# A two-pass transformer layer on one core: the turn of the first value block is put later, and the last SwiGLU step is cut down to its bank-freeing adds

## The chip, the core and the metric

The kernel runs on one core of one Trainium2 chip. The number that counts is the device time of one execution, in microseconds (us). The kernel before the change took 1397.57 us (median of 3 runs, 1396.01 to 1397.66).

The engines are named as the profile names them: PE is TensorE, which does the matmuls; PEld is its weight loading; DVE is VectorE, ACT is ScalarE, POOL is GpSimd, and SP is the queue from which nearly all transfers between memory and the core are issued. Each engine works through its own list of instructions in order; an instruction waits until what it reads is written and until the buffer that it writes is free. All tiles lie in the core's main memory, SBUF, but for the matmuls' results: these go into eight banks of a smaller one, PSUM, each 128 by 512 numbers of 32 bits. A bank can be written afresh only when another engine has read out what lay in it.

## The reference

One layer with 1024 tokens and 1024 features. With the sizes of this case only the first of the two kinds of attention is run:

```
h = x
hn = rms_norm(h, norm_mix);  h = h + stick_breaking_attention(hn, sb_w_in, sb_w_out)
h = h + (silu(a) * b) @ ffn_w_out      where a, b = split(rms_norm(h, norm_ffn) @ ffn_w_in)
gate = sigmoid(rms_norm(h, norm_ple) @ ple_w_gate)
h = h + gate * (p @ ple_w_proj)
return rms_norm(h, final_norm)

# stick-breaking attention, 16 heads of 64, strictly causal:
#   A[t,s] = sigmoid(z_ts) * prod over s<j<t of (1 - sigmoid(z_tj)),   out = A @ v
```

The SwiGLU's inner width is 2816, which is 22 blocks of 128.

## The kernel before, in words

Everything is kept transposed: features lie on the 128 partitions, tokens along the rows, in two halves of 512. Every matmul operand is split into a high part (a rounded cast, made by ACT) and a low part (the rest, a subtraction on DVE or POOL), and each product is three matmuls: high by high, high by low, low by high (`mm3`, lines 126 to 129). For weights this is `w_split` (line 98): line 106 casts on ACT, and line 107 picks the engine that subtracts in line 108.

**The attention** goes over 8 pairs of heads. While the attention of one pair is computed, the projections of the next pair (queries, keys, values: `sel` 0, 1, 2, each in two halves `h`) are fed in between, a few matmuls at a time, by the generator `proj_steps` (line 321). One step of it is one `mm3`; eight steps (`kt` 0 to 7) fill a bank of the kind `b_pj`, which DVE then reads out. The values of a pair are first turned by PE, 128 by 128 at a time: `turn_v` (line 308) does four such turns with the unit matrix into a bank `b_tp` (line 314), and ACT and DVE copy the result into the tile `V` (lines 317, 318). What is turned is `dv`, a difference of neighbouring values that DVE makes in line 305. These turns are not issued at once: they are put on the list `late`, and `proj_steps` empties the list when it comes to `kt == 3`, whichever block that is in. The banks `b_tp` and the score banks `b_z` share one ring of four. The scores are made by `s_atom` (PE in lines 407 and 408, the sigmoid on ACT in line 410, a scan on DVE in line 417), and the probabilities are turned by `a_atom` (PE in line 430, ACT and DVE in lines 439 and 440).

**The SwiGLU's first product** goes over 22 steps `k`, each with seven products of four `mm3` (a Strassen-like scheme that saves one in eight): `ps1`, `ps5`, `ps6`, `ps7`, `ps2`, `ps4` and `ps3`, in this order on PE, each in a bank of its own out of eight in a ring (`mb`). DVE adds them up into the tiles `q1`, `u2`, `u4` and `c22` (line 634, `add`); an add that reads a product from its bank frees that bank. The four sums are multiplied by the norm's factor (line 828, `scaled`, on DVE or POOL), and `glu` (line 830) makes silu(a) times b of two of them at a time: a sigmoid on ACT (832), two products on DVE (833, 834), and a store to memory from SP (835). `glu` of the second token half runs one step later, as `tail`.

**The second product** follows directly: for each half of the tokens, 22 out steps, each with eight `mm3`, one into each of eight banks (`pm[0]` to `pm[7]`). An out step needs the block's weights, split by `w_split`, and the stored activations, loaded again (`act_dma`) and split (`act_split`: cast in line 626, subtraction in line 627). The first two weight blocks and the first two activations are split within the last SwiGLU step, `k == NFF - 1`, so that out step 0 can begin when the last product is done. The ring of banks goes on across this border: the third group of out step 0 takes the bank of `ps5`, the sixth that of `ps2`, the seventh that of `ps4`, and the eighth that of `ps3`.

All of this is written out by hand in one order (no scheduler), from the second product of the attention on.

Of the kernel before, what the change touches and what calls it, by code (L numbers as in the profile page):

```python
# [19 lines left out]
NFF = 22  # L20
# [20 lines left out]
def tile_trunk(ctx: ExitStack, tc: tile.TileContext, xT, pT, gains, ident, w_qkv, w_o, w_fi, w_fo, w_g, w_p, outT):  # L41
# [54 lines left out]
    def w_split(k):  # L96
        if k < lim[0] and k in raws:
            n = order[k][1]
            t = raws.pop(k)
            if len(order[k]) > 2 and order[k][2]:  # L100
                hi = xp.tile([P, T], F32R, name=f"whi{k}", tag="X").rearrange("p (k m) -> p k m", k=KT)
                lo = xp.tile([P, T], F32R, name=f"wlo{k}", tag="X").rearrange("p (k m) -> p k m", k=KT)
            else:
                hi = wp.tile([P, KT, P], F32R, name=f"whi{k}", tag="whi", bufs=2)
                lo = wp.tile([P, KT, P], F32R, name=f"wlo{k}", tag="wlo", bufs=2)
            nc.scalar.copy(hi[:, :n, :], t[:, :n, :])  # L106
            eng = nc.gpsimd if k < N1 or k >= len(order) - 3 else nc.vector
            eng.tensor_tensor(lo[:, :n, :], t[:, :n, :], f(hi[:, :n, :]), op=ALU.subtract)  # L108
            parts[k] = (hi, lo)

# [58 lines left out]
    with ExitStack() as c1:  # L169
# [152 lines left out]
        def proj_steps(pr, sels=(0, 1, 2)):  # L322
            for sel in sels:
                wh, wl = w_next()
                if sel == 0:
                    alloc_qk(pr)
                for h in range(2):
                    hs = slice(h * 512, h * 512 + 512)
                    ps = jb()
                    for kt in range(KT):  # L330
                        if kt == 3:
                            while late:
                                late.pop(0)()
                        mm3(ps, wh[:, kt, :], wl[:, kt, :], xh[kt][:, hs], xl[kt][:, hs], kt == 0, kt == KT - 1)
                        if kt == KT - 1:
                            if sel == 0:
                                evac_q(pr, ps, h)
                            elif sel == 1:
                                evac_k(pr, ps, h)
                            else:  # L340
                                v = evac_v(pr, ps, h)
                                late.append(lambda pr=pr, v=v, h=h: turn_v(pr, v, h))
                        yield
# [278 lines left out]
    def act_split(i):  # L622
        if i < 2 * NFF and i not in acts:
            t = araw.pop(i)
            a = duo(xp, f"act{i}", "X", None)
            nc.scalar.copy(a[:, 0, :], t)
            nc.vector.tensor_tensor(a[:, 1, :], t, f(a[:, 0, :]), op=ALU.subtract)
            acts[i] = a

    with ExitStack() as c2:  # L630
# [196 lines left out]
        def scaled(t, h, eng=nc.vector):  # L827
            eng.tensor_tensor(t, t, rstd2[:, HS[h]], op=ALU.mult)  # L828
# [14 lines left out]
        for k in range(NFF):  # L843
            w = wc
            wc, todo = fi_prep(k + 1)
            fi_load(k + 2)
            if k >= NFF - 2:
                for i in range(2):
                    w_load(n_fi + 2 * (k + 2 - NFF) + i)
                act_dma(k + 2 - NFF)  # L850
            ps1 = prod(w["A11"], "B11")
            q1 = tmp("q1")
            nc.scalar.copy(q1, ps1)
            if tail:
                tail()
            ps5 = prod(w["S1"], "T1")
            if k == 0:
                ps2 = prod(w["A12"], "B21")
            if k:
                todo[0]()  # L860
                todo[1]()
            ps6 = prod(w["S2"], "T2")
            u2 = tmp("u2")
            add(u2, ps6, q1)
            u4 = tmp("u4")
            add(u4, ps5, u2)
            if k:
                todo[2]()
            if k == NFF - 1:
                act_split(0)  # L870
                w_split(n_fi)
            ps7 = prod(w["S3"], "T3")
            add(u2, ps7, u2)
            c22 = tmp("c22")
            add(c22, ps5, u2)
            if k == 0:
                yy = stats_sum(cp, mb(), acc2, 0, KT)
                for q in range(3):
                    todo[q]()
            todo[3]()  # L880
            if k:
                ps2 = prod(w["A12"], "B21")
            add(q1, ps2, q1)
            if k:
                scaled(c22, 1, nc.gpsimd)
                scaled(q1, 0)
            todo[5]()
            if k == NFF - 1:
                act_split(1)
            ps4 = prod(w["A22"], "T4")  # L890
            add(u2, ps4, u2)
            if k:
                scaled(u2, 0, nc.gpsimd)
            todo[4]()
            if k:
                glu(k, 0, q1, u2)
            if k == NFF - 1:
                w_split(n_fi + 1)
                act_dma(2)
            ps3 = prod(w["S4"], "B22")  # L900
            if k == 0:
                for h in range(2):
                    stats_spread(mb(), yy[:, 4 * h:4 * h + 4], rstd2, 512 * h, 4)
                scaled(c22, 1, nc.gpsimd)
                scaled(q1, 0)
                scaled(u2, 0, nc.gpsimd)
                glu(k, 0, q1, u2)
            add(u4, ps3, u4)
            scaled(u4, 1)

            def tail(k=k, u4=u4, c22=c22):
                glu(k, 1, u4, c22)

        tail()


    p3 = ctx.enter_context(tc.tile_pool(name="p3", bufs=1, reuse_waits="tile"))
# [26 lines left out]
    for h in range(2):  # L944
        pm = [None] * KT
        tail = []
        for k in range(NFF):
            i = h * NFF + k
            act_dma(i)
            act_split(i)  # L950
            act_dma(i + 1)
            act_dma(i + 2)
            wh, wl = w_next()
            if h == 1 and 2 <= k < 10:
                parts3(k - 2, 0)
            act_split(i + 1)
            a = acts.pop(i)
            if h == 1 and k in WGK:
                wg.append(w_next())
            if k < NFF - 2:  # L960
                for m in range(KT):
                    if k == 0:
                        pm[m] = mb()
                    mm3(pm[m], wh[:, m, :], wl[:, m, :], a[:, 0, :], a[:, 1, :], k == 0, False)
            else:
                tail.append((wh, wl, a))
        res = []
        for m in range(KT):
            t = tmp("h2")
            nc.sync.dma_start(t, h2_d[m][h])  # L970
            res.append(t)
        for m in range(KT):
            for q, (wh, wl, a) in enumerate(tail):
                mm3(pm[m], wh[:, m, :], wl[:, m, :], a[:, 0, :], a[:, 1, :], False, q == 1)
            residual(m, h, pm[m], res[m])
# [139 lines left out]
```

## Time and profile before

| what | value |
|---|---|
| median of 3 runs | 1397.57 us |
| the profiled execution's own time | 1397.2 us |
| its span, first to last instruction | 1395.4 us |
| PE busy | 1359.3 us, 97% of the span |
| DVE busy | 1006.8 us, 72% |
| ACT busy | 609.2 us, 44% |
| POOL busy | 406.4 us, 29% |
| granted PE clock, mean | 0.993 of full speed |

The profile is of one execution. An engine counts as busy while an instruction of its own runs. The timeline lists instructions by their start; in brackets stands how long the engine had been idle and who let it go on. The granted clock is the share of full speed at which PE was allowed to run in a stretch: 1.0 is 2.4 GHz, 0.5 is 1.2 GHz. Starts of PE's matmuls lie closer together than their durations, since they are pipelined; what counts is the distance from one start to the next.

### The profile page before, as it was taken

What the parts mean: (1) busy time and instruction counts of PE and PEld (TensorE: products, weight loads), DVE (VectorE), ACT (ScalarE), POOL (GpSimd) and SP (SyncE); (2) the same over time, 40 slices, a digit from 0 to 9 for tenths busy, and PEclk for the clock granted to TensorE, in tenths of its full rate; (3) what the DMA queues carried; (4) which work ended last, traced back from release to release, by engine and by line L of the source; (5) the groups of instructions that cost most, each with busy time, mean ns of one, the idle gap of its engine ahead of it and who ended that gap; (6) DMA issues with size and microseconds to landing.
All of it is one profiled execution on the core that took longest, in us unless ns stands there. A gap on an engine that the chain in (4) does not pass through costs nothing. (4 is left out here: it accounts for less than half of the span.)

```text
span 1395.4 us, 17612 instructions
## 1 busy us (share of the span) xinstructions
PE 1359.3 (97%) x6620; PEld 1135.1 (81%) x6620; DVE 1006.8 (72%) x1305; ACT 609.2 (44%) x1082; POOL 406.4 (29%) x280
## 2 busy tenths in 40 slices
PE   8899999999999999999999999999999999999996
PEld 6788888888888878878888888888877888888896
DVE  6778788787887875677888888888884336645775
ACT  6555665655566664443232323222322223433333
POOL 2221322312222501234445444545440000301321
PEclk9999999999999999999999999999999999999998
DMA  5101111111111571442221222221235445555123
GB/s 188 41 31 46 46 46 46 46 34 43 46 46 61 182 263 46 162 146 79 91 85 58 84 91 91 91 71 66 91 106 188 138 156 208 168 175 181 31 71 104
DMA packets 55509, 137.54 MB, mean 99 GB/s; under 512 B 6016, under 2 KB 10496, under 8 KB 55424
## 3 DMA queue, kind: packets, MB, share of 16 engines
q1 hardware_dynamic: 53136, 128.82, 27.1%
q0 software_dynamic: 2016, 7.34, 1.5%
q8 instruction: 52, 0.85, 0.3%
q14 instruction: 33, 0.27, 0.1%
q10 hardware_dynamic: 272, 0.26, 0.1%
HBM read 104.94 MB, written 31.46 MB: 98 GB/s over the span
## 5 line engine op out<-in xcount | busy, mean ns | idle before, releaser
L417 DVE TENSOR_TENSOR_SCAN a<-a,hot 128x128 f32<-128x128 f32 (+7 forms) x128 | 191.7, 1515 | 29.4 <-ACT a L410 28.9
L108 DVE TENSOR_TENSOR wlo<-wraw,whi 128x1024 fp32r<-128x1024 f32 x57 | 71.6, 1256 | 124.4 <-ACT whi L106 124.3
L106 ACT CAST whi<-wraw 128x1024 fp32r<-128x1024 f32 x84 | 88.2, 1051 | 165.2 <-PE b_m L128 144.8
L108 POOL TENSOR_TENSOR wlo<-wraw,whi 128x1024 fp32r<-128x1024 f32 x27 | 67.6, 2509 | 297.6 <-ACT whi L106 141.5
L127 PE MATMUL b_pj<-xh,whi 128*128 128x512 f32 x352 | 141.1, 401 | 0.0
L129 PE MATMUL b_pj<-xh,wlo 128*128 128x512 f32 x352 | 139.1, 395 | 0.4 <-POOL wlo L108 0.4
L128 PE MATMUL b_pj<-xl,whi 128*128 128x512 f32 x352 | 138.5, 393 | 0.0
L440 DVE TENSOR_TENSOR al<-b_tp,ah 128x512 fp32r<-128x512 f32 (+2 forms) x160 | 93.1, 599 | 51.3 <-ACT ah L439 50.9
L439 ACT CAST ah<-b_tp 128x512 fp32r<-128x512 f32 (+2 forms) x160 | 81.9, 522 | 78.4 <-PE b_tp L430 77.5
L410 ACT ACTIVATE a<-b_z 128x128 f32<-128x128 f32 (+2 forms) x192 | 86.8, 490 | 56.5 <-PE b_z L408 55.5
L127 PE MATMUL b_m<-act,whi 128*128 128x512 f32 x264 | 104.0, 394 | 3.5 <-DVE u L634 3.4
L129 PE MATMUL b_m<-act,wlo 128*128 128x512 f32 x264 | 103.8, 393 | 0.2 <-DVE wlo L108 0.2
L128 PE MATMUL b_m<-act,whi 128*128 128x512 f32 x264 | 103.7, 393 | 0.0
L430 PE MATMUL b_tp<-hot,a 128*128 128x128 f32 x576 | 94.2, 272 | 2.6 <-DVE al L440 2.6
L430 PEld LDWEIGHTS b_tp<-hot,a 128*128 128x128 f32 x576 | 72.8, 140 | 25.6 <-DVE al L440 5.6
L129 PEld LDWEIGHTS b_pj<-xh,wlo 128*128 128x128 f32 x352 | 66.3, 188 | 16.3 <-POOL wlo L108 0.5
L128 PEld LDWEIGHTS b_pj<-xl,whi 128*128 128x128 f32 x352 | 66.5, 189 | 9.2
L127 PEld LDWEIGHTS b_pj<-xh,whi 128*128 128x128 f32 x352 | 66.5, 189 | 9.1
L450 PE MATMUL b_av<-ah,V 128*128 128x512 f32 (+2 forms) x160 | 70.7, 442 | 0.0
L941 POOL TENSOR_TENSOR acc<-acc,sq 128x512 f32<-128x512 f32 x10 | 17.6, 1758 | 161.4 <-ACT sq L939 160.7
L832 ACT ACTIVATE sg<-u 128x512 f32<-128x512 f32 x22 | 13.9, 632 | 111.2 <-issue 86.4
L127 PEld LDWEIGHTS b_m<-act,whi 128*128 128x128 f32 x264 | 50.1, 190 | 15.1 <-DVE u L634 4.2
(3039 smaller groups left out, 3746.9 us busy)
## 6 DMA issues: line engine op xcount, KB each, us to landing
fraw<-w_fi SPq DMA_DIRECT2D x44, 512.0 KB, 4.1
wraw<-w_fo SPq DMA_DIRECT2D x44, 512.0 KB, 3.6
wraw<-w_qkv SPq DMA_DIRECT2D x22, 512.0 KB, 3.6
araw<-act SPq DMA_DIRECT2D x44, 256.0 KB, 3.9
h<-h SPq DMA_DIRECT2D x32, 256.0 KB, 3.7
sp<-hl SPq DMA_DIRECT2D x14, 512.0 KB, 3.0
act<-u SPq DMA_DIRECT2D x22, 256.0 KB, 2.2
act<-c SPq DMA_DIRECT2D x22, 256.0 KB, 2.6
```

Source lines behind the costliest of these rows:

```text
L106: nc.scalar.copy(hi[:, :n, :], t[:, :n, :])
L108: eng.tensor_tensor(lo[:, :n, :], t[:, :n, :], f(hi[:, :n, :]), op=ALU.subtract)
L127: nc.tensor.matmul(ps, whi, xhi, start=first, stop=False)
L128: nc.tensor.matmul(ps, whi, xlo, start=False, stop=False)
L129: nc.tensor.matmul(ps, wlo, xhi, start=False, stop=last)
L410: nc.scalar.activation(a[:, c0:c0 + e], z[:, :e], AF.Sigmoid, scale=-SCALE)
L417: nc.vector.tensor_tensor_scan(a[:, L - 1::-1], a[:, L - 1::-1], hot[:, back], 0.0, op0=ALU.mult, op1=ALU.max)
L430: nc.tensor.transpose(b[:, j * P:(j + 1) * P], a[:, kt * P:(kt + 1) * P], idn)
L439: nc.scalar.copy(ah[:, m0:m0 + 512 - j0 * P], b[:, j0 * P:])
L440: nc.vector.tensor_tensor(al[:, m0:m0 + 512 - j0 * P], b[:, j0 * P:], f(ah[:, m0:m0 + 512 - j0 * P]), op=ALU.subtract)
L450: nc.tensor.matmul(ps[:, c0:], o.V[:, kt, hd, :], ah[:, r0:], start=kt == 0, stop=False)
L941: eng.tensor_tensor(acc3[:, hs], acc3[:, hs], s, op=ALU.add)
```

## The change

Three edits, in the attention's first pair and at the border between the SwiGLU's two products.

```diff
# w_split: which engine makes the low part
-            eng = nc.gpsimd if k < N1 or k >= len(order) - 3 else nc.vector
+            eng = nc.gpsimd if k < N1 or n_fi <= k < n_fi + 2 or k >= len(order) - 3 else nc.vector
# proj_steps: when the waiting turns are issued
-                        if kt == 3:
+                        if kt == 3 and (pr > 1 or sel or h):
# the SwiGLU's step k
             if k == NFF - 1:
+                w_split(n_fi)
                 act_split(0)
-                w_split(n_fi)
...
-            if k:
+            if 0 < k < NFF - 1:
                 scaled(c22, 1, nc.gpsimd)
                 scaled(q1, 0)
             todo[5]()
             if k == NFF - 1:
+                w_split(n_fi + 1)
                 act_split(1)
             ps4 = prod(w["A22"], "T4")
             add(u2, ps4, u2)
-            if k:
+            if 0 < k < NFF - 1:
                 scaled(u2, 0, nc.gpsimd)
             todo[4]()
-            if k:
+            if 0 < k < NFF - 1:
                 glu(k, 0, q1, u2)
             if k == NFF - 1:
-                w_split(n_fi + 1)
                 act_dma(2)
...
             add(u4, ps3, u4)
-            scaled(u4, 1)
+            if k < NFF - 1:
+                scaled(u4, 1)
...
-        tail()
+        def rest_0(q1=q1, u2=u2):
+            scaled(q1, 0)
+            scaled(u2, 0)
+            glu(NFF - 1, 0, q1, u2)
+
+        def rest_1(u4=u4, c22=c22):
+            scaled(u4, 1)
+            scaled(c22, 1)
+            glu(NFF - 1, 1, u4, c22)
+
+        rests = [rest_0, rest_1]
# the out steps, at the end of each
+            if k and rests:
+                rests.pop(0)()
```

First place, the start of the attention. PE's list, a piece of the difference (- before, + now); `whi`/`wlo` are pair 1's query weights, `KA` and `QA` the keys and queries of pair 0, `dv` the values to be turned. Left out at the `@@` line are the rest of the first half block, the scores of query blocks 0 to 3 and nine projection matmuls of the second half, which are the same in both:

```order
 L129 MATMUL b_pj<-xh_197,wlo_318 128x512
-L314 MATMUL b_tp<-hot,dv 128x128 x8
 L127 MATMUL b_pj<-xh_215,whi_317 128x512
 L128 MATMUL b_pj<-xl_216,whi_317 128x512
@@ -191,4 +190,5 @@
 L407 MATMUL b_z<-KA_407,QA_405 128x320
 L408 MATMUL b_z<-KLA_136,QA_405 128x320
+L314 MATMUL b_tp<-hot,dv 128x128 x8
 L127 MATMUL b_pj<-xh_215,whi_317 128x512
```

The eight turns stood after the 9th matmul of pair 1's first block; now they stand after all 24 of it, the scores of the first five query blocks, and 9 matmuls of the second half. ACT's two casts into `V` and DVE's two subtractions move with them: on DVE from before the read-out of the first half block (line 282) to behind the scan of the fifth query block, ahead of that of the sixth.

Second place, the last SwiGLU step. DVE's list before, from the first activation's low part on (34 and 35 are the out steps' first two weight blocks, `q1_9331`, `u2_9364`, `u4_9366`, `c22_9389` the last step's four sums, `b_m` and `b_pj` the banks):

```order
L627 TENSOR_TENSOR act0_9368<-araw_9164,act0_9368 128x512
L108 TENSOR_TENSOR wlo34_9372<-wraw34_9160,whi34_9371 128x1024
L634 TENSOR_TENSOR u2_9364<-b_pj_9375,u2_9364 128x512
L634 TENSOR_TENSOR c22_9389<-b_m_9338,u2_9364 128x512
L634 TENSOR_TENSOR q1_9331<-b_m_9391,q1_9331 128x512
L828 TENSOR_TENSOR q1_9331<-q1_9331,rstd2_6118 128x512
L627 TENSOR_TENSOR act1_9407<-araw_9316,act1_9407 128x512
L634 TENSOR_TENSOR u2_9364<-b_m_9410,u2_9364 128x512
L833 TENSOR_TENSOR q1_9331<-q1_9331,sg_9425 128x512
L834 TENSOR_TENSOR u2_9364<-q1_9331,u2_9364 128x512
L108 TENSOR_TENSOR wlo35_9431<-wraw35_9162,whi35_9430 128x1024
L634 TENSOR_TENSOR u4_9366<-b_m_9436,u4_9366 128x512
```

The same number of rows of the changed kernel, from the same instruction on:

```order
L627 TENSOR_TENSOR act0_9372<-araw_9164,act0_9372 128x512
L634 TENSOR_TENSOR u2_9364<-b_pj_9375,u2_9364 128x512
L634 TENSOR_TENSOR c22_9389<-b_m_9338,u2_9364 128x512
L634 TENSOR_TENSOR q1_9331<-b_m_9391,q1_9331 128x512
L627 TENSOR_TENSOR act1_9409<-araw_9316,act1_9409 128x512
L634 TENSOR_TENSOR u2_9364<-b_m_9412,u2_9364 128x512
L634 TENSOR_TENSOR u4_9366<-b_m_9428,u4_9366 128x512
L936 TENSOR_SCALAR gf_9472<-gn_67 128x8
L108 TENSOR_TENSOR wlo36_9511<-wraw36_9312,whi36_9510 128x1024
L627 TENSOR_TENSOR act2_9514<-araw_9426,act2_9514 128x512
L828 TENSOR_TENSOR q1_9331<-q1_9331,rstd2_6118 128x512
L828 TENSOR_TENSOR u2_9364<-u2_9364,rstd2_6118 128x512
```

The add that reads the last product (`u4`) was the 12th row and is the 7th. Two low parts of weights, one scaling and two products of `glu` no longer stand ahead of it: the low parts are on POOL, the others come behind the split for out step 2.

POOL's list at the same place, a piece of the difference:

```order
 L828 TENSOR_TENSOR u_9225<-u_9225,rstd_6118 128x512
 L689 TENSOR_TENSOR wc21A_9289<-fraw_1_9012,wc21A_9289 128x512
-L828 TENSOR_TENSOR c_9389<-c_9389,rstd_6118 128x512
-L828 TENSOR_TENSOR u_9364<-u_9364,rstd_6118 128x512
-L941 TENSOR_TENSOR acc_9484<-acc_9484,sq 128x512 x7
+L108 TENSOR_TENSOR wlo_9369<-wraw_9160,whi_9368 128x1024
+L108 TENSOR_TENSOR wlo_9406<-wraw_9162,whi_9405 128x1024
+L952 TENSOR_TENSOR acc_9470<-acc_9470,sq 128x512 x7
```

POOL gives up two scalings of the last step and gets the two low parts. On SP the first store of the last step's results (first token half) stood ahead of the activations for out step 2; it now stands behind the activations of out steps 2 and 3 and the weights of step 4, and ahead of the activations of step 4 and the weights of step 5. The second store stands behind these and ahead of the activations of step 5.

## Rows read from the trace of the kernel before

**Rows 1.** the page's busy time of each engine: us, share of the span, instructions.
```profile
PE 1359.3 (97%) x6620; PEld 1135.1 (81%) x6620; DVE 1006.8 (72%) x1305; ACT 609.2 (44%) x1082; POOL 406.4 (29%) x280
```

**Rows 2.** waits of PE: who waited, for whom; us in total, times, longest.
```profile
PE b_tp L314 <- DVE dv L305: 5.3, 3, 2.1
...
PE b_m L127 <- DVE u L634: 3.4, 2, 3.2
```

**Rows 3.** timeline of PE, first place: start, duration, work [idle before <-releaser].
```profile
45.16 0.39 PE L127 MATMUL b_pj<-xh,whi 128*128 128x512 f32 x1
...
46.97 0.39 PE L129 MATMUL b_pj<-xh,wlo 128*128 128x512 f32 x1
49.16 0.63 PE L314 MATMUL b_tp<-hot,dv 128*128 128x128 f32 x4 [1.80 <-DVE dv L305]
51.91 1.12 PE L314 MATMUL b_tp<-hot,dv 128*128 128x128 f32 x4 [2.13 <-DVE dv L305]
52.68 0.78 PE L127 MATMUL b_pj<-xh,whi 128*128 128x512 f32 x1
...
57.32 0.28 PE L407 MATMUL b_z<-KA,QA 128*128 128x256 f32 x1
...
64.75 0.60 PE L430 MATMUL b_tp<-hot,a 128*128 128x128 f32 x4
65.10 0.48 PE L127 MATMUL b_pj<-xh,whi 128*128 128x512 f32 x1
```

**Rows 4.** busy time by stretch: us, PE, PEld, DVE, ACT, POOL, PEclk, DMA, GB/s.
```profile
52.68:55.27 2.59, 2.59 (x8) 2.07 (x7) 0.69 (x1) 0.59 (x1) 0.00 (x0) 0.53 0.51 185
...
1049.09:1055.22 6.13, 6.13 (x14) 4.78 (x15) 3.87 (x6) 2.10 (x3) 0.00 (x0) 0.50 0.48 150
```

**Rows 5.** timeline of DVE, first place.
```profile
49.65 2.21 DVE L305 TENSOR_TENSOR dv<-vf 128x512 f32<-128x512 f32 x1
51.78 0.68 DVE L318 TENSOR_TENSOR V<-b_tp,V 128x512 fp32r<-128x512 f32 x1
...
57.59 0.69 DVE L282 TENSOR_TENSOR qf<-b_pj,rstd 128x512 f32<-128x512 f32 x1 [3.22 <-PE b_pj L129]
...
60.67 5.21 DVE L417 TENSOR_TENSOR_SCAN a<-a,hot 128x384 f32<-128x384 f32 x4
```

**Rows 6.** timeline of POOL, first place.
```profile
48.96 2.34 POOL L108 TENSOR_TENSOR wlo<-wraw,whi 128x1024 fp32r<-128x1024 f32 x1 [0.49 <-ACT whi L106]
```

**Rows 7.** timeline of PE, second place.
```profile
1039.54 0.39 PE L127 MATMUL b_m<-act,whi 128*128 128x512 f32 x1
...
1049.09 0.79 PE L127 MATMUL b_m<-act,whi 128*128 128x512 f32 x1 [3.23 <-DVE u L634]
...
1055.47 0.40 PE L127 MATMUL b_pj<-act,whi 128*128 128x512 f32 x1
```

**Rows 8.** timeline of ACT, second place.
```profile
1035.71 0.60 ACT L626 CAST act<-araw 128x512 fp32r<-128x512 f32 x1
1036.22 1.05 ACT L106 CAST whi<-wraw 128x1024 fp32r<-128x1024 f32 x1
```

**Rows 9.** timeline of DVE, second place.
```profile
1036.57 0.69 DVE L834 TENSOR_TENSOR c<-u,c 128x512 f32<-128x512 f32 x1
...
1038.50 0.68 DVE L627 TENSOR_TENSOR act<-araw,act 128x512 fp32r<-128x512 f32 x1
...
1040.24 0.68 DVE L634 TENSOR_TENSOR u<-b_pj,u 128x512 f32<-128x512 f32 x1
...
1048.35 0.68 DVE L634 TENSOR_TENSOR u<-b_m,u 128x512 f32<-128x512 f32 x1
```

**Rows 10.** timeline of POOL, in the step before the last.
```profile
1024.34 1.29 POOL L689 TENSOR_TENSOR wc21S<-s,wc21S 128x512 fp32r<-128x512 f32 x1 [3.26 <-PE b_m L129]
```

**Rows 11.** timeline of DVE, in the step before the last.
```profile
1024.80 0.68 DVE L634 TENSOR_TENSOR q<-b_m,q 128x512 f32<-128x512 f32 x1
```

**Rows 12.** DMA issues on the page: KB each, median us from issue to landing.
```profile
araw<-act SPq DMA_DIRECT2D x44, 256.0 KB, 3.9
```

## The prediction

> **What bounds the kernel now.** I read the page's table of engines first: PE is busy for 1359.3 of 1395.4 us [rows 1], so a change pays only where it closes a gap of PE or raises its clock. The waits of PE come next; two of the largest are those that the edits touch: 5.3 us of turns that waited for `dv`, and 3.4 us of matmuls that waited for a sum of line 634 [rows 2]. The timeline of PE puts each in its place, and the busy times by stretch show what else was lost there: PE's granted clock.
>
> First place: the nine matmuls ahead of the turns start 0.226 us apart (45.16 to 46.97, eight distances). Then PE is idle for 1.80 us, turns half of the values, is idle for another 2.13 us, turns the rest, and goes on at 52.68 [rows 3]. In the stretch behind it, 52.68 to 55.27, the granted clock is 0.53, so PE ran there at the lower level, 1.2 GHz, for nearly all of it [rows 4]. The cause is that `dv` is late: DVE's second one starts at 49.65 and takes 2.21 us [rows 5], because POOL works on a low part from 48.96 for 2.34 us [rows 6]; DVE ends 0.56 us after POOL does.
>
> Second place: the first out matmul starts at 1039.54, the one that opens the eighth group at 1049.09 after 3.23 us of idleness [rows 7]. Its bank is freed by DVE's add at 1048.35 [rows 9], though the product was there before 1039.54. DVE is what ends last. From 1049.09 to 1055.22 the granted clock is 0.50: all of it at 1.2 GHz [rows 4].
>
> **First part: the turns later.** From 45.16 to the first score matmul at 57.32 pass 12.16 us. The work in it is 24 matmuls at 0.226 us, 5.42 us, and two groups of four turns, each 0.35 us at full clock (a like group starts at 64.75 and the next matmul at 65.10 [rows 3]), 0.70 us. So 12.16 - 6.12 = 6.04 us are lost, by idleness and by clock. Nothing is removed but this loss. In the new order PE runs the 24 matmuls to 50.58, then scores, whose keys and queries DVE writes ahead of `dv`. When the turns come up, at about 54.5, `dv` has been ready since 51.86.
>
> What is late next is DVE. Its work from the read-out in line 282 to the end of four scans runs without a gap from 57.59 to 65.88, 8.29 us [rows 5]. Now it can begin at 51.86, when the second `dv` is made. The two subtractions into `V` (0.68 us each) come ahead of the last of these scans, which has 768 of the four scans' 2304 columns: 1.74 of 5.21 us. So the first subtraction ends at 51.86 + 8.29 - 1.74 + 0.68 = 59.09. It frees the bank that the first probability turns write. PE wants that bank 7.43 us behind its first score (64.75 - 57.32), plus the two groups of turns: 50.58 + 7.43 + 0.70 = 58.71. I put a new wait of 0.4 us there. Net 5.6 us. Bounds: 6.0 without the new wait; 3.2 if the scan that is delayed also meets POOL's next low part and has to stand still for 2.4 us, as `dv` did. ACT's casts into `V` hide in its gaps. I take the value near the upper end, since DVE was idle for 3.22 us ahead of the read-out at 57.59 [rows 5], which gives it room.
>
> **Second part: only bank-freeing adds in the last step.** From 1039.54 to 1055.47 PE issues 36 matmuls, 8.14 us at 0.226, in 15.93 us: 7.79 us lost [rows 7].
>
> The new DVE order up to the add of `u4` drops two weight low parts, a scaling and two products. POOL makes the low parts. The first weight cast now stands ahead of the activation's on ACT, so it starts at 1035.71 and, at 1.05 us, ends at 1036.76 [rows 8]. POOL begins in earnest when DVE's product at 1036.57 is over, at 1037.26 [rows 9], and needs 2.34 us: 1039.6. DVE's subtraction for activation 0, ready at 1038.50, reads two tiles in SBUF as `dv` does, so it waits for POOL and ends 0.56 us later, about 1040.2. PE's second matmul, due at 1039.77, starts 0.4 us late. The adds follow at 0.7 us: `u2` 1040.9, `c22` 1041.6, which the third group awaits at 1041.3 (0.25 us lost), `q1` 1042.2. POOL's second low part runs from 1040.2 to 1042.5, the subtraction for activation 1 ends at 1043.1, `u2` at 1043.8, `u4` at 1044.4. PE opens the eighth group at 1039.54 + 0.65 + 21 x 0.226 = 1044.9. So it no longer waits, with 0.5 us to spare, and nothing lets the clock fall. Gain 7.79 - 0.65 = 7.1 us. Bounds: 7.8 without any new wait; 4.1 if the clock falls all the same (15 distances from 1049.09 took 6.38 us in place of 3.39, so 3.0 us).
>
> The adds themselves read a bank, and the trace shows such an add untouched by POOL: 0.68 us at 1024.80 [rows 11], inside POOL's 1.29 us from 1024.34 [rows 10]. The Trainium skill's page "SBUF — State Buffer", section "SBUF: two separate sides", says that the port pair shared by VectorE and GpSimd is an exclusive lock held for the whole instruction, and that of VectorE's instructions those with two SBUF inputs contend for it. By that rule moving low parts to POOL is dear for the two activation splits, and free for the adds; the trace agrees on both (2.21 us for `dv`, 0.68 us for the add). Without the lock the 0.4 us at the second matmul would go, and the sum would be 13.1 instead of 12.7.
>
> What moved behind: the scalings and `glu` of the last step go to the ends of out steps 1 and 2, behind the splits for steps 2 and 3 on DVE and ACT, each step with 5.4 us (24 x 0.226), of which the splits take 1.65 us on ACT [rows 8] and on DVE no more than POOL's 2.34 and 0.68, 3.0 us. The split for step 2 starts when step 0's matmuls are done, at 1045.7; the first results are out at about 1051.7 and the second at 1057. The store of the first stands ahead of activation 4 on SP; with 3.9 us to land [rows 12] that arrives near 1056 and is needed at about 1060. So this costs nothing; the cover is 4 us.
>
> **The sum.** 5.6 + 7.1 = 12.7 us. The profiled execution took 1397.2 us, 1.8 us more than its span, and the median of the runs is 0.4 us higher. 1397.2 - 12.7 = 1384.5; for a median, 1384.9. The likeliest case's own range, from the bounds (3.2 + 4.1 = 7.3 and 6.0 + 7.8 = 13.8 off 1397.57): 1383.8 to 1390.3.
>
> **The rivals.**
> 1. DVE hands the first place's gain back. It has no gap in those 8.29 us, and if the two subtractions push it behind POOL's next low part, 2.4 us return: 1387.3. Against it: that low part starts only when PE has finished the second half block, so it shifts as PE does.
> 2. The second place keeps a stall. If the adds, too, stood still while POOL works, `c22` would end at about 1043.9 and the third group lose 2.3 us more; with the clock's 3.0 us, 5.3 us: 1390.2. For it: gaps of 1.80 and 2.13 us sufficed to lower the clock at the first place. Against it: the add at 1024.80.
> 3. The change does not do what it says in one half: PE's wait there was for another thing that comes just as late (the loaded activation 1, say). Then only 5.6 or 7.1 us go: 1390.5 or 1392.
> 4. No change: what PE gains is waited off later, at a transfer that keeps its own time, 1395 to 1398. Against it: all of PE's idleness is 1395.4 - 1359.3 = 36 us, a fifth of it (7.2 us in three gaps) at these two places, and the loads are issued as buffers come free, which PE's progress decides.
> 5. Slower: the stores on SP hold back the loads of out steps 4 and 5. This decides from the point where the results come more than 4 us later than I reckon (after 1056 and 1061); a microsecond later is then a microsecond of idle PE, twice, each with the clock's 3.0 us. At 4 us beyond the point: 2 x (4 + 3.0) = 14.0, against 12.7 gained: 1399. For it: each result now waits for two more splits. Against it: DVE's splits leave 2.4 of the 5.4 us of a step free.
>
> **How the numbers follow.** Forecast 0.66, rival 1 0.13, rival 2 0.10, rival 3 0.03, rival 4 0.04, rival 5 0.04. 0.2% of the time, 2.8 us, is about what a measurement of this kernel can tell from no change. Faster by more: the forecast and rivals 1 to 3, 0.92; same: 0.04; slower: 0.04. The range takes the likeliest case and rivals 1 and 2, with the spread of the runs (1.6 us to the lower side) at the low end: 1382.5 to 1391.
>
> **What would show it.** In the new profile: no wait of turns for `dv` near 50 us, score matmuls from about 50.6, a granted clock of 1.0 there; a wait of some 0.4 us ahead of the first probability turns near 59; at the border, a first low part on POOL of about 2.4 us, the eighth group's bank free about 5 us after the first out matmul, and a granted clock of 1.0 through it. A gap of over 1 us ahead of the third or the eighth group, or a clock of 0.5, would refute the second part; a DVE that frees the first `b_tp` bank later than PE by 2 us would refute the first; PE idle in out steps 4 and 5 would speak for rival 5.

## The result and the profile after

The kernel with the change took 1385.74 us (median of 4 runs, 1385.05 to 1389.32), the one before 1397.62 us (4 runs, 1396.01 to 1399.11). The ratio is 0.992, with a 95% interval of 0.99 to 0.9941: 11.9 us less. The profiled execution took 1385.05 us with a span of 1383.3 us, 12.1 us less than the span before. All times below that are set against rows of before are taken from these two executions.

The page's busy times come first, as in [rows 1]:

```profile
PE 1355.3 (98%) x6620; PEld 1133.4 (82%) x6620; DVE 1005.5 (73%) x1305; ACT 608.9 (44%) x1082; POOL 408.3 (30%) x280
```

PE has as many instructions as before, was busy for 4.0 us less (it ran fewer of them at half clock), and idle for 28.0 us in place of 36.1. PE's waits (who waited, for whom; us in total, times, longest) show which gaps went. This is the list of after that answers to [rows 2]:

```profile
PE b_z L127 <- ACT whi_s L233: 5.0, 1, 5.0
...
PE b_pj L127 <- ACT plt L513: 1.6, 1, 1.6
PE b_tp L314 <- DVE dv L305: 1.4, 1, 1.4
PE b_m L128 <- DVE xc3T L637: 1.1, 1, 1.1
...
PE b_m L135 <- DVE acc L1021: 0.4, 1, 0.4
```

Of the turns' three waits for `dv` one is left, of 1.4 us; the two at the start of the attention are gone. The waits for a sum of line 634 are no longer in the list. The last row is new: a short wait at the very end.

The first place, timeline of PE in after (start, duration, work), as in [rows 3]:

```profile
50.60 0.28 PE L407 MATMUL b_z<-KA,QA 128*128 128x256 f32 x1
...
54.55 1.04 PE L314 MATMUL b_tp<-hot,dv 128*128 128x128 f32 x8
...
59.00 0.66 PE L430 MATMUL b_tp<-hot,a 128*128 128x128 f32 x4
```

The scores start at 50.60 instead of 57.32, and the eight turns run in one piece with no idleness ahead of them. DVE beside it, as in [rows 5]:

```profile
49.68 2.25 DVE L305 TENSOR_TENSOR dv<-vf 128x512 f32<-128x512 f32 x1
...
58.28 1.26 DVE L318 TENSOR_TENSOR V<-b_tp,V 128x512 fp32r<-128x512 f32 x2
```

`dv` is as late as it was (2.25 us from 49.68), but nothing waits for it. The first subtraction into `V` ends at 58.28 + 0.68 = 58.96, and the probability turns that take its bank start at 59.00.

The second place, timeline of PE in after, as in [rows 7]:

```profile
1033.66 0.39 PE L127 MATMUL b_m<-act,whi 128*128 128x512 f32 x1
1034.12 0.50 PE L128 MATMUL b_m<-act,whi 128*128 128x512 f32 x1
...
1035.45 0.50 PE L127 MATMUL b_m<-act,whi 128*128 128x512 f32 x1
...
1039.00 0.39 PE L127 MATMUL b_m<-act,whi 128*128 128x512 f32 x1
...
1042.40 0.39 PE L127 MATMUL b_pj<-act,whi 128*128 128x512 f32 x1
```

The eighth group opens 5.34 us after the first out matmul (9.55 before), with no wait ahead of it, and the 36 matmuls take 8.74 us in place of 15.93. DVE beside it, as in [rows 9]:

```profile
1032.50 1.57 DVE L627 TENSOR_TENSOR act<-araw,act 128x512 fp32r<-128x512 f32 x1
1033.99 0.68 DVE L634 TENSOR_TENSOR u<-b_pj,u 128x512 f32<-128x512 f32 x1
...
1035.31 0.68 DVE L634 TENSOR_TENSOR q<-b_m,q 128x512 f32<-128x512 f32 x1
1035.91 0.97 DVE L627 TENSOR_TENSOR act<-araw,act 128x512 fp32r<-128x512 f32 x1
1036.81 1.27 DVE L634 TENSOR_TENSOR u<-b_m,u 128x512 f32<-128x512 f32 x2
```

POOL makes the two low parts in the same stretch:

```profile
1030.88 5.45 POOL L108 TENSOR_TENSOR wlo<-wraw,whi 128x1024 fp32r<-128x1024 f32 x2 [3.67 <-issue]
```

The two follow each other without a break and end at 1036.33. The two activation splits, which read only SBUF, are stretched (1.57 and 0.97 us; the first out step's was 0.68 in [rows 9]); the adds that read a bank keep 0.68 us with POOL at work beside them. The last row of DVE holds the adds of `u2` and `u4`; it ends at 1038.08, 0.9 us before PE wants the bank.

The busy times by stretch (us, PE, PEld, DVE, ACT, POOL, PEclk, DMA, GB/s) over both places, before:

```profile
45.00:57.32 12.32, 8.39 (x34) 6.57 (x33) 8.05 (x9) 4.69 (x7) 3.62 (x2) 0.86 0.15 44
1039.54:1055.47 15.93, 12.19 (x37) 8.50 (x36) 12.14 (x17) 4.29 (x6) 2.95 (x2) 0.79 0.26 86
```

and after:

```profile
45.00:57.32 12.32, 12.32 (x64) 10.60 (x63) 12.13 (x15) 8.00 (x15) 3.70 (x2) 1.00 0.14 44
1033.66:1042.40 8.74, 8.67 (x37) 6.60 (x36) 6.08 (x10) 2.20 (x3) 2.67 (x1) 1.00 0.34 133
```

The granted clock is full in both. In the first place's 12.32 us PE now gets through 64 instructions where it had got through 34.

Not all of it arrives at the end. The timeline of PE at the tail, before:

```profile
1380.87 0.28 PE L129 MATMUL b_m<-gh,wlo 128*128 128x256 f32 x1
1381.21 0.38 PE L135 MATMUL b_m<-ones,acc 128*128 128x1 f32 x2
1384.20 0.38 PE L137 MATMUL b_m<-ones,sq 128*128 128x1 f32 x2 [2.61 <-ACT sq L1003]
```

and after:

```profile
1367.76 0.28 PE L129 MATMUL b_m<-gh,wlo 128*128 128x256 f32 x1
1368.45 0.38 PE L135 MATMUL b_m<-ones,acc 128*128 128x1 f32 x2 [0.41 <-DVE acc L1021]
1371.44 0.59 PE L137 MATMUL b_m<-ones,sq 128*128 128x1 f32 x2 [2.61 <-ACT sq L1016]
```

The last main matmul comes 13.11 us earlier, the end only 12.1. The first small sum waits 0.41 us for DVE, and the sums behind the 2.61 us gap run at half clock (0.59 us against 0.38).

The whole account, from first instruction to last:

| stretch | before | after | gain |
|---|---|---|---|
| to the first out matmul | 1039.54 | 1033.66 | 5.88 |
| the 36 matmuls at the border | 15.93 | 8.74 | 7.19 |
| from there to the last main matmul | 325.40 | 325.36 | 0.04 |
| tail | 14.53 | 15.54 | -1.01 |
| span | 1395.4 | 1383.3 | 12.1 |

### The profile page after: what moved, and what is told of

Same layout as the page of the kernel before. It is cut to its first block, busy times and chain, and to the rows that moved or that the text cites. A ratio compares the mean times of both kernels' runs of the same rounds, so it can differ in the third digit from the quotient of the medians.

```text
span 1383.3 us, 17608 instructions
## 1 busy us (share of the span) xinstructions
PE 1355.3 (98%) x6620; PEld 1133.4 (82%) x6620; DVE 1005.5 (73%) x1305; ACT 608.9 (44%) x1082; POOL 408.3 (30%) x280
## 5 line engine op out<-in xcount | busy, mean ns | idle before, releaser
L108 POOL TENSOR_TENSOR wlo<-wraw,whi 128x1024 fp32r<-128x1024 f32 x29 | 72.7, 2513 | 295.7 <-ACT whi L106 121.6
```

## The experiments

Eleven kernels ran in three groups, each beside the kernel before on the same chip. In the first its median was 1397.38 us (14 runs), in the second 1397.13 us (21 runs), in the third 1397.59 us (9 runs). Ratios are to these, with the 95% interval in brackets.

### The turns alone

```diff
-                        if kt == 3:
+                        if kt == 3 and (pr > 1 or sel or h):
```

> The later turns alone, the border as before. Theory (the first place loses 6.0 us by two gaps and PE's lower clock, and gives nearly all of it back): 5.6 to 5.8 us faster, about 1391.8 against 1397.5; the score matmuls begin at 50.6 in place of 57.3, and the last SwiGLU step begins 5.7 us earlier with its 3.2 us gap and its stretch at half clock as before. Rival (the gain of the turns is waited off later, at transfers with their own time): under 3 us, and the border's first out matmul comes less than 3 us earlier.

Measured: 1391.21 us (5 runs, 1390.99 to 1393.05), ratio 0.9959 [0.9945, 0.9973], 6.2 us faster. In its profiled execution PE was busy for all of 45.00 to 57.32, at a clock of 1.00. The border still had its gap there, but a smaller one, and PE needed 12.87 us for the 36 matmuls; timeline of PE:

```profile
1044.32 0.50 PE L127 MATMUL b_m<-act,whi 128*128 128x512 f32 x1 [2.81 <-DVE u L634]
```

The place itself behaves as forecast: the first score comes at 51.09, 5.44 us behind the first of the nine matmuls (45.65), as in the change. But the 6.2 us are no clean measure of it. PE's first out matmul came at 1036.60, only 2.94 us earlier than before, not 5.7. That is the sign that the rival named, though not for its reason: no wait at a transfer is new, but the clock fell near 629, where it stayed full in the profile of before; busy times by stretch:

```profile
628.00:634.00 6.00, 5.65 (x18) 4.18 (x18) 5.18 (x16) 1.02 (x3) 1.05 (x1) 0.72 0.51 165
```

DVE had not lost that time. Its add of `u4` ended at 1044.27, 4.8 us earlier than before, so that PE got most of its loss back in the smaller gap at the border. A further 1.2 us of the gain is a shorter stretch at half clock behind that gap (15 distances take 5.15 us in place of 6.38), at a place that the first edit does not touch.

### The border alone

```diff
-                        if kt == 3 and (pr > 1 or sel or h):
+                        if kt == 3:
```

(against the changed kernel: all edits but the first)

> The border's two edits alone (low parts on POOL, the last step's products put off), the turns as before. Theory: about 7.2 us faster, 1390.3; the gaps of 1.8 and 2.1 us at the turns stay, and no gap of over 0.5 us is left at the border. With the run of the turns alone the two gains add up to that of the whole change. Rival (the two halves share a limit): the sum of the two differs from 12 us by more than 2.

Measured: 1392.36 us (4 runs, 1390.72 to 1393.32), 0.9963 [0.9948, 0.9978], 5.0 us faster, 2 us less than expected. The trace tells why. Its busy times by stretch:

```profile
51.00:58.00 7.00, 5.24 (x15) 4.31 (x16) 2.99 (x3) 0.85 (x2) 1.15 (x1) 0.51 0.26 75
628.00:636.00 8.00, 6.22 (x27) 5.07 (x26) 6.80 (x10) 4.01 (x7) 2.95 (x3) 0.79 0.48 167
1036.00:1052.00 16.00, 16.00 (x72) 13.23 (x72) 12.05 (x18) 5.38 (x8) 5.47 (x2) 1.00 0.51 181
```

At the border PE is busy without a break at full clock, and from its first out matmul (1042.85) to the end pass 348.7 us, where before took 355.9: the 7.2 us expected. They were in part offset ahead of the border, in code that is the same as before: the clock fell at the turns for about twice as long as in [rows 4], and once more near 631. At the very start this execution had lost 0.85 us more than the one of before (its nine matmuls begin at 46.01, not 45.16). The mechanism holds; the size, by the median, is blurred by where the clock falls in an execution. The two halves add up to 6.2 + 5.0 = 11.2 us, within 2 us of 12, so the rival is out.

### Only the move to POOL

```diff
-            eng = nc.gpsimd if k < N1 or k >= len(order) - 3 else nc.vector
+            eng = nc.gpsimd if k < N1 or n_fi <= k < n_fi + 2 or k >= len(order) - 3 else nc.vector
...
+                w_split(n_fi)
                 act_split(0)
-                w_split(n_fi)
...
+                w_split(n_fi + 1)
                 act_split(1)
...
-                w_split(n_fi + 1)
                 act_dma(2)
```

> Only the move of the two low parts to POOL (with the casts ahead of the activations' as in the change); scalings and products of the last step stay where they were. Theory (what counts is what stands ahead of the adds on DVE, and the SBUF splits stand still while POOL works): no gain; the eighth group's bank is freed at about 1050.2 on the time of before, 1 us later than before, by POOL's four instructions and the splits between them; 1397 to 1400. Rival (the low parts' 2.4 us on DVE were what held the banks back): 2 to 5 us faster.

Measured: 1397.53 us (10 runs), 1.0003 [0.9994, 1.0013]: no gain. Timeline of PE:

```profile
1047.67 0.80 PE L127 MATMUL b_m<-act,whi 128*128 128x512 f32 x1 [2.26 <-DVE u L634]
...
1050.73 0.80 PE L127 MATMUL b_m<-act,whi 128*128 128x512 f32 x1 [1.41 <-DVE u L634]
```

and of DVE:

```profile
1039.42 1.57 DVE L627 TENSOR_TENSOR act<-araw,act 128x512 fp32r<-128x512 f32 x1
...
1044.16 2.85 DVE L627 TENSOR_TENSOR act<-araw,act 128x512 fp32r<-128x512 f32 x1
...
1049.38 0.69 DVE L834 TENSOR_TENSOR u<-q,u 128x512 f32<-128x512 f32 x1 [1.17 <-POOL u L828]
1049.99 0.68 DVE L634 TENSOR_TENSOR u<-b_m,u 128x512 f32<-128x512 f32 x1
```

What DVE saves by not making the low parts (two of 1.22 us) it loses by standing still beside POOL: the two activation splits take 1.57 and 2.85 us, where each took 0.68 before. Its wait of 1.17 us for a scaling on POOL is not new; the kernel before had the same one, ahead of 1046.61. The eighth bank came free 9.99 us behind the first out matmul, 0.5 us later than before (9.49), where 1 us had been expected. One gap of 3.23 us became two of 2.26 and 1.41.

### Only the putting off

The opposite half: the scalings, `glu` and stores of the last step put off as in the change, both low parts left on DVE at their old places.

```diff
-            eng = nc.gpsimd if k < N1 or n_fi <= k < n_fi + 2 or k >= len(order) - 3 else nc.vector
+            eng = nc.gpsimd if k < N1 or k >= len(order) - 3 else nc.vector
```

(against the border alone, the calls of `w_split` back in their places)

> Only the putting off: the low parts stay on DVE at their old places, the scalings and products of the last step go behind out steps 1 and 2. Theory: DVE's add of u4 comes about 8 us earlier than before even with two low parts of 1.2 us ahead of it, the eighth group loses some 0.3 us at most, the clock stays up: 6.5 to 7 us faster, 1390.7, within 1 us of the run with both border edits. Rival (POOL's help is needed): a gap of 2 us or more is left ahead of the eighth group and the clock falls: under 4 us faster.

Measured: 1391.66 us (4 runs, 1390.56 to 1392.48), 0.9958 [0.9944, 0.9973]: 5.7 us faster, within 1 us of the border alone, but short of the 6.5 to 7 expected. Timeline of DVE:

```profile
1042.76 0.68 DVE L627 TENSOR_TENSOR act<-araw,act 128x512 fp32r<-128x512 f32 x1
...
1043.96 1.21 DVE L108 TENSOR_TENSOR wlo<-wraw,whi 128x1024 fp32r<-128x1024 f32 x1
1045.10 0.68 DVE L634 TENSOR_TENSOR u<-b_m,u 128x512 f32<-128x512 f32 x1
```

With POOL silent the split takes 0.68 us and a low part 1.21. The eighth bank is free at 1045.78, and PE opens that group at 1045.83, 5.50 us behind its first out matmul at 1040.33. Behind that first out matmul the bank is free 4.0 us sooner than before (5.45 us, 9.49 before), not 8 as expected, and that suffices. So the putting off is what closes the gap, and the move to POOL adds only slack: 0.9 us in the change, 0.05 here.

### Idle matmuls in the gaps

Two kernels with the order of before, and matmuls put into the gaps whose results go unused or add zero: eight and ten at the turns, fourteen ahead of the eighth group. They shorten no wait; they only keep PE at work.

```diff
                         if kt == 3:
-                            while late:
-                                late.pop(0)()
+                            if pr == 1 and sel == 0 and h == 0:
+                                idle = tb()
+                            for n in (8, 10):
+                                if pr == 1 and sel == 0 and h == 0:
+                                    for q in range(n):
+                                        nc.tensor.matmul(idle, wh[:, 3, :], xh[3][:, hs], start=True, stop=True)
+                                if late:
+                                    late.pop(0)()
# the other kernel, at the border; zr is all zero
+                    if i == 0 and m == KT - 1:
+                        for q in range(14):
+                            nc.tensor.matmul(pm[m - 1], zr, a[:, 0, :], start=False, stop=False)
```

> The kernel before with 8 and 10 matmuls more, whose result is not used, in PE's two gaps at the turns: the waits for dv stay, only PE is not idle in them. Theory (part of the 6.0 us lost there is clock, not waiting): no stretch at half clock there, and from the first added matmul to the first score matmul 1.6 us less than before although the gaps' length stays; the whole 1.6 to 3 us faster, 1395. Rival (the clock's loss is nothing of its own: PE is only late): no change or slower by the added matmuls.

> The kernel before with 14 matmuls with a weight of zeros, which add nothing, ahead of the eighth group of out step 0, in the 3.2 us gap. Theory: DVE frees the bank when it did, but no stretch at half clock follows: 1.7 to 3 us faster, 1395. Rival: the clock falls all the same or the time does not move.

Measured: at the turns 1394.02 us (10 runs), 0.9979 [0.997, 0.9988], 3.1 us faster; at the border 1395.4 us (10 runs), 0.9988 [0.9979, 0.9997], 1.7 us faster. The busy times by stretch of the first:

```profile
45.00:57.32 12.32, 12.30 (x58) 9.78 (x57) 8.60 (x9) 5.62 (x9) 4.55 (x3) 1.00 0.15 45
```

and of the second:

```profile
1036.00:1056.00 20.00, 20.00 (x90) 16.57 (x89) 17.06 (x25) 6.39 (x9) 2.96 (x2) 1.00 0.37 127
```

With the gaps filled, the clock stays full: part of each loss was clock, part waiting, as the prediction took it. The sizes are only rough: at the turns the trace shows 1.3 us gained at the place itself (10.83 us from the first of the nine matmuls to the first score, 12.16 before), less than the 3.1 of the medians. At the border the 36 matmuls took 11.33 us. That is 4.6 us less than in the profile of before, but the added matmuls account for only a part of it: in this execution the clock fell near 637, PE came later, and DVE freed the bank 7.70 us behind the first out matmul, not 9.49. In the two other profiles with the old border where that distance is as short (turns alone 7.67, matmuls at the turns 7.74) the 36 matmuls took 12.87 and 12.94 us; against these 1.5 us are gained, close to the 1.7 of the medians. Neither comes near the 6.2 and 5.0 us of the edits that take the wait itself away.

### Two more gaps

Can the same treatment close what is left? The last pair's second turn of values, which still waits 1.4 us for `dv`, was put two steps later in the projection of `p`, and among the splits of the SwiGLU's inputs for the last feature block (`T2`, `T3` and `T4` are sums of them) `T2` was put first, so that PE's matmul near 622 waits less.

```diff
-                            while late:
+                            while late and (m4 or m or h):
...
+                if m == 7:
+                    x = xc(j, "T2")
+                    nc.scalar.copy(x[:, 0, :], t2)
+                    sub(x[:, 1, :], t2, f(x[:, 0, :]))
...
-                src = (("T2", t2), ("T3", t3), ("T4", t4))
+                src = (("T2", t2), ("T3", t3), ("T4", t4))[m == 7:]
```

Both together, and the change once more beside it:

> The changed kernel with two more gaps of PE treated in the same way: the last pair's second value turn waits for dv (1.39 us at 467), so it is issued two steps later; and the third group of the SwiGLU's first step waits for the low part of T2 (1.1 to 1.8 us near 622, and in two runs so far a stretch of 3.4 us at half clock followed), so that DVE now makes this low part ahead of T3 and T4. Theory: both gaps go, 2.5 us at least off the changed kernel and the runs scatter less: 1383 against 1385.7. Rival (DVE is the bound there, so the wait turns up at the next instruction): within 1 us of the changed kernel.

> The changed kernel again, on the same chip as the three others: 1385 to 1386.5, and the share of runs in which the clock falls near 622 (each such fall costs 1.7 us by its length at half clock).

Measured: both together 1388.83 us (5 runs, 1387.64 to 1389.36), 0.9939 [0.9925, 0.9952]; the change again 1385.56 us (4 runs, 1385.14 to 1387.83), 0.9919 [0.9906, 0.9933]. By the medians the two edits cost 3.3 us; the two intervals overlap a little. PE's waits of the two-gap kernel:

```profile
PE b_pj L127 <- ACT plt L513: 3.5, 1, 3.5
...
PE b_m L127 <- ACT wc0A L686: 1.1, 1, 1.1
```

The wait for `dv` is gone and that for `xc3T` is not among those of 0.4 us or more, but the next waits are as long. The clock fell at both of them; busy times by stretch:

```profile
494.00:497.50 3.50, 2.66 (x8) 2.35 (x9) 1.55 (x4) 2.70 (x7) 0.00 (x0) 0.61 0.57 214
...
628.00:634.00 6.00, 4.46 (x13) 3.30 (x14) 4.75 (x14) 1.96 (x4) 1.28 (x1) 0.77 0.61 175
```

In neither of the two profiles of the change did it fall between 20 us and 1370 us. In how many executions it falls near 622 stays open: each kernel has the clock by stretch of one execution only. Each half was then run alone:

> The change, with the splits of T2 put ahead of those of T3 and T4 for the last feature block (m == 7) of the attention's output product, the second half of the study's two-gap kernel alone. Theory: the two-gap kernel lost its 3.3 us mainly at the other half (the value turn of the last pair), and this half only trades waits: the wait for xc3T near 622 us (1.1 to 1.8 us) goes down to about 0.1, and waits for wc0A near 628 and 630 us of 1.1 and 0.6 us come in its place; time within 0.5 us of the change, 1385.1 to 1386.1. Rival: the new waits near 630 us lower the clock, as in the two-gap kernel (0.63 us matmuls there); then about 1.7 us slower, 1387.3. Second rival: the gain of the first wait stays (1.5 us): 1384.2.

> The change, with the last pair's second value turn put behind the gate's first projection block, the first half of the two-gap kernel alone. Theory: the wait for dv (1.4 us) goes, and the wait for plt near 494 us grows from 1.6 to about 3.5 us, one gap in place of two, with a stretch of half clock behind it; that costs 2 to 3.3 us: 1387.5 to 1388.8. Rival: one gap of 3.5 us is as good as two that sum to 3.0, and the two-gap kernel's loss is at its other half near 630 us: then within 0.6 us of the change, 1385.6 to 1386.2.

Measured: `T2` first 1387.59 us (5 runs), 0.9928 [0.9915, 0.994]; the values later 1387.4 us (5 runs), 0.9926 [0.9913, 0.9939]. Each was 10.0 to 10.2 us faster than the kernel before beside it, where the change was 11.6 faster and both edits together 8.3: about 1.5 us lost by each. The intervals overlap the change's, so that neither loss is certain alone; a gain is not in sight for either. For `T2` first the first rival comes nearest: in its profile the wait near 622 is 0.28 us, one of 1.10 us turns up at 628, and behind it the clock is at half; busy times by stretch:

```profile
628.00:634.00 6.00, 5.78 (x13) 4.09 (x14) 5.08 (x16) 1.14 (x3) 1.28 (x1) 0.50 0.47 169
```

The values later met neither expectation. The wait for `plt` did not grow (1.40 us); the time came back as a wait of scores at 480; timeline of PE:

```profile
480.49 0.42 PE L407 MATMUL b_z<-KA,QA 128*128 128x320 f32 x1 [1.25 <-DVE al L440]
...
494.19 0.50 PE L127 MATMUL b_pj<-ph,whi 128*128 128x512 f32 x1 [1.40 <-ACT plt L513]
```

1.25 + 1.40 us, where the change had 1.39 for `dv` and 1.56 for `plt`. This profile is of the fastest of the five executions (1385.68 us), so it does not show what the median lost. What the 3.5 us in the two-gap kernel's one profile came from stays open.

### The change without POOL

The change with the low parts back on DVE at their old places (the first edit and the putting off), the calls of `w_split` back in their places too.

```diff
-            eng = nc.gpsimd if k < N1 or n_fi <= k < n_fi + 2 or k >= len(order) - 3 else nc.vector
+            eng = nc.gpsimd if k < N1 or k >= len(order) - 3 else nc.vector
```

> The change without its move of two weight low parts to POOL: they are made by DVE at their old places, the turns later and the last step's scalings and products put off stay. Theory: DVE has 1.22 us for a low part where POOL has 2.4, and with three vector instructions and two products taken out of its list it still frees the eighth bank in time; the border has no gap of over 0.5 us and a granted clock of 1.0, and the time is within 0.7 us of the change: 1385.0 to 1386.4. Rival: the move is needed, since both DVE low parts (2.4 us) stand ahead of the adds; the eighth group then waits 1 us or more with a lower clock behind it: 1387.5 or over.

Measured: 1386.75 us (5 runs, 1385.29 to 1388.11), 0.992 [0.9906, 0.9934], the change's own ratio, though 0.35 us above the range expected. In its profile PE's first out matmul came 2.2 us later than in the change's (1035.87 against 1033.66); most of that was lost before 500 us, far ahead of what this edit touches (a wait for `plt` of 2.0 us, not 1.56, and a clock of 0.61 over 494.00 to 497.50). The 36 matmuls at the border take 9.20 us (8.74 in the change), and the clock stays at 1.00; the busy times by stretch:

```profile
1035.87:1044.00 8.13, 7.81 (x33) 5.65 (x32) 6.26 (x10) 3.15 (x4) 0.00 (x0) 1.00 0.46 145
```

At the border the theory holds: two of the three parts of the second edit, the move and the places of `w_split`, could be left out. No version that ran beats the change.

## Why the prediction was right

**The first place.** It said 6.04 us lost, 0.4 given to a new wait, net 5.6. PE's time to the first out matmul is 5.88 us shorter. The scores started at 50.60 (50.58 forecast). The new limit is where it was put: DVE's first subtraction into `V` ended at 58.96 (59.09 forecast) and PE came for the bank at 59.00. PE needed 8.40 us from the first score to there (8.13 forecast), so that the wait of 0.4 us all but vanished: none is listed. The edit alone, run by itself, gave 6.2 us, of which its profile puts 1.2 at the border. Rival 1 is out: DVE did not give the gain back.

**The second place.** It said 7.79 us lost, 0.65 left in two short waits, net 7.1; it was 7.19. (It also has the eighth group's product there before 1039.54; that product's last matmul started at 1039.32 and ended at 1039.71, which changes nothing in the sum.) The second matmul was 0.23 us late (0.4 forecast), the third a further 0.11, the third group less than 0.1 (0.25); the eighth group opened 5.34 us behind the first (5.40), with 0.9 us to spare (0.5). The Trainium skill's page "SBUF — State Buffer", section "SBUF: two separate sides", has the port pair of VectorE and GpSimd as a lock held for a whole instruction, and VectorE's instructions with two SBUF inputs contending for it. The traces agree on both sides: 1.57, 0.97 and 2.85 us for splits beside POOL's low parts, 0.68 with POOL silent, and 0.68 for adds from a bank under POOL's second low part. Rival 2, adds that stand still too, is out by these rows.

**Which part did it.** The prediction put the two low parts on POOL and the dropped scaling and products into one sum. The runs take them apart: the move alone is worth nothing (1.0003), the putting off alone as much as both. The sum was right; a reader of it could have thought the move necessary, and it is not.

**Where luck helped.** Both losses were read from one execution, and neither is the same in the next one. With the old order of the turns, four other profiles (the border alone, only the move, only the putting off, the matmuls at the border) need 12.3 to 13.5 us from the first of the nine matmuls to the first score, where the profile of before needed 12.16; three of them need over 13. With the old border, two other profiles need 12.87 and 12.94 us for the 36 matmuls, where it needed 15.93: so 4.7 and 4.8 us were lost there, not 7.79. In both of these the clock had fallen near 629 or 635 and PE came late at the border, where it would have waited for DVE anyway. The first term was thus rather small and the second large for a typical execution, and in the sum the two errors partly cancel. The medians of the halves run alone point the same way (6.2 for 5.6, 5.0 for 7.1), but each is uncertain by some 2 us.

**What moved behind.** It said that this costs nothing. The stretch from the border to the last main matmul took 325.36 us against 325.40, and the list of waits has none of out steps 4 and 5. The stores were issued by SP 11.7 and 17.1 us behind the first out matmul (12.2 and 17.5 forecast). Rivals 4 and 5 are out, and with a gain at both places rival 3.

**What it missed.** The sum was 12.7 us, the trace has 12.1, the medians 11.9. The two places gave 0.4 us more than said, and the tail took 1.01 back: 0.41 us of waiting for a statistic that DVE adds up, and the last small sums at half clock. Three of the six profiles with the turns later and the last step's work put off have this wait (the change, the change again, the values later), and in these three DVE had itself waited 0.34 or 0.35 us for a sum on POOL shortly before; the other three have neither. Why it comes and goes stays open. No term of the sum covered this place, whose work the change does not touch.

## What to carry to other kernels

Where PE waits for a bank, read the list of the engine that frees it, and take out of that list, ahead of the freeing instruction, whatever no one needs yet; moving such work to another engine is worth less, and nothing at all where the two engines get in each other's way. Where PE waits for an operand and other matmuls are ready, a later place costs nothing, but only if the next operand down the line is early; if it is just as late, the gap only moves. Judge a closed gap by the time between two fixed instructions on either side of it, since the rest of the program can hide or imitate some microseconds in any one run. And read the size of a loss from more than one execution before it goes into a sum: the same border cost 7.8 us in one and 4.7 in another.

## What the runs showed of the hardware that was not expected

Like gaps cost unlike amounts of clock. At the turns, with the same two gaps of 1.80 and 2.12 us, the clock was 0.51 over 51.00 to 58.00 in the border-alone kernel; before had 0.53 over a stretch of 2.59 us [rows 4], and was at full speed ahead of the first score. Ahead of the eighth group a gap of 3.23 us was followed by 0.50 over 6.13 us [rows 4], one of 2.81 us in the kernel with the turns alone by 0.72 over six:

```profile
1044.00:1050.00 6.00, 5.68 (x18) 4.52 (x19) 4.15 (x7) 2.08 (x3) 0.00 (x0) 0.72 0.48 145
```

A gap of 1.10 us at 628 in the kernel with `T2` first was followed by 0.50, as shown above, and one of 1.14 us at 621.69 in the change by no loss at all:

```profile
621.00:627.00 6.00, 5.31 (x31) 4.71 (x32) 4.84 (x7) 2.97 (x7) 2.22 (x2) 1.00 0.34 119
```

At one and the same place it differs too. The matmul near 622 waited 1.77 us both in the change run again and in the kernel with the values later, whose code is the same there; the clock was 1.00 behind it in the first and fell in the second:

```profile
621.00:627.00 6.00, 5.18 (x31) 4.62 (x32) 4.96 (x7) 2.98 (x7) 2.09 (x2) 1.00 0.38 115
```

```profile
622.00:626.00 4.00, 3.52 (x10) 2.81 (x11) 3.92 (x5) 1.06 (x3) 1.64 (x1) 0.66 0.28 112
```

The mean granted clock of the change's four runs goes with their times: 0.996 at 1385.05 us, 0.995 at 1385.23 and 1386.26, 0.993 at 1389.32. Four runs prove little, but they fit with the rows above: where the clock falls in an execution is part of the scatter of a few microseconds, which hides what a trace shows at one place. What such a fall costs depends on what comes next. With the old border PE got most of it back, as it had to wait there for DVE (turns alone, above); in the change there is no such wait to absorb it.
